# Two transformer blocks with expert layers: the gates' one-hots in token pairs, and every gate through DRAM

## The chip, the cores and the metric

One NeuronCore of one Trainium2 chip runs the whole program in one launch. Its engines work side by side, each through its own queue in order: TensorE (PE, with its weight loads PEld) multiplies matrices into PSUM, VectorE (DVE) and ScalarE (ACT) work elementwise on SBUF and PSUM, GpSimd (POOL) on SBUF, and SyncE (SP) and ScalarE issue DMAs. The metric is the device time of one execution in microseconds; before the change it is 2398.7 us, the median of 3 runs (2398.04 to 2399.11).

## What is computed

Two transformer blocks over 256 tokens of width 1024. The change lies in the expert layer of the second block, which runs twice (`li` = 0 and 1):

```python
def peer(h, wq, keys, u_tab, v_tab):           # for each block of 128 tokens
    q = (hblk @ wq).reshape(PEER_BLOCK, P_HEADS, 2, D_KEY_HALF)
    s = jnp.einsum('nhpd,hpkd->nhpk', q, keys)
    top_s, top_i = lax.top_k(s, P_TOPK)         # 16 of 128, for two halves of 8 heads
    cand_s = (top_s[:, :, 0, :, None] + top_s[:, :, 1, None, :]).reshape(...)
    cand_i = (top_i[:, :, 0, :, None] * N_KEYS + top_i[:, :, 1, None, :]).reshape(...)
    best_s, best_pos = lax.top_k(cand_s, P_TOPK)
    idx = jnp.take_along_axis(cand_i, best_pos, axis=-1)
    gate = jax.nn.softmax(best_s, axis=-1)
    act = jax.nn.gelu(jnp.einsum('nd,nhkd->nhk', hblk, u_tab[idx]))
    return jnp.einsum('nhk,nhkd->nd', gate * act, v_tab[idx])
```

Each token picks 16 experts of 128 x 128 = 16384 for each of 8 heads.

## The kernel before

Instead of gathering rows of U and V, the kernel multiplies the whole tables. The 16384 experts are 128 tiles of 128: tile `e` holds the experts of one first index, the second index lies on the partitions. For a **U tile** (`a_tile`, L1441) TensorE multiplies a 128 x 1024 tile of U with all 256 tokens, in 8 pieces of 128 rows; for a **V tile** (`v_tile`, L1468) it multiplies the gated activations of 128 experts with a 128 x 1024 tile of V into four PSUM banks `acc`. Between them lies `A[g]`, eight groups of 16 tiles: Gelu (L1453) writes it, the gates are multiplied into it, `w_pair` (L1459) splits two tiles of it for the V matmuls.

Everything is done in split precision: `hilo` (L200 to L202) makes a high half on ScalarE (L201) and a low half on VectorE or GpSimd (L202), and each product is three matmuls (L225 to L227 for U, with 256 columns; L242, L244, L246 for V, with 512). A weight tile is loaded on SP into one of 5 `raw` buffers (L197), split into one of 3 `hi` and `lo` buffers two tiles ahead, then used. `_plan` fixes the order of the tiles, U 0 to 111, V 0 to 15, U 112 to 127, V 16 to 127, and says which are split on GpSimd ("pool"): of U the five in `U_POOL0`.

**Gates** are dense: for each token a 128 x 128 matrix of gate values over first and second index, made of its 128 picks (they lie on the partitions) as a product of two one-hots. `g_hot` (L1379) takes four tokens: one VectorE instruction (L1382) compares the picks' two indices with `iota4`, a second (L1384) multiplies the first one-hot with the gate's high and low f16 part. Its tile has the order (kind, index, token), so that the columns of one token's one-hot lie four f16 apart. `g_mm` multiplies (L1392, L1393: for each of 4 tokens a high and a low product of 128 columns, both with the same weights). `g_out` evicts: first indices 0 to 63 stay in SBUF, 64 to 127 go to the DRAM tile `gspill` over ScalarE's DMA queue (L1406). `g_times` (L1408) multiplies gates into `A`.

**What sets the order** is a list by hand. Work for VectorE is put on `fill_q` with a cost in credits; after each tile `fill(budget)` adds a budget (at most 4.0 is kept) and runs entries while the credit is positive; `fill_all` runs what is left. In the Q stage (nine calls with 2.6) top-16 entries of 2.1 come in, 16 in all. Then `queue_topk` adds candidates (2.0 and 0.5), 8 times best of 1.4, 0.3, 18 pick steps of 1.8 (`pick_eq` on VectorE L1329 and GpSimd L1331, `pick_sum` L1334), decode 2.5 and transposes 0.5. U tiles 1 to 63 give 1.6 each and carry these; U tiles 64 to 111 give 2.75 and carry 67 gate steps of 1.9 (`queue_g0`: step i makes one-hots i, multiplies i - 1, evicts i - 2, and every second step multiplies 8 tokens of the first half into `A`); V tiles 16 to 63 carry 17 steps that read `gspill` back, 16 tokens each, and multiply the second half. In layer 0 `pump` also advances a generator that loads modulation rows (`ada`, L320 on VectorE, 512 KB each; its input row holds a `t4` buffer): after every second tile from U tile 36 to 63, of V 0 to 15, U 112 to 127 and V 64 to 111. `t4` has 4 buffers of 4 KB a partition; one-hots, rows read back and long-lived rows share them.

Of the kernel before, what the change touches and what calls it, by code (L numbers as in the profile page):

```python
# [19 lines left out]
P = 128  # L20
# [60 lines left out]
def _plan(t):  # L81
# [10 lines left out]
    for li in range(2):  # L92
# [7 lines left out]
        def u(a, b):  # L100
            return [(("u", li, e), t["u"][li, e], "pool" if e in U_POOL or e in U_POOL0 else None) for e in range(a, b)]

        def v(a, b, offload=()):
            return [(("v", li, e), t["v"][li, e], "pool" if e in offload else BIG[e % 2] if e >= P - TAIL else None) for e in range(a, b)]

        p += u(0, 112) + v(0, 16) + u(112, 128) + v(16, 64, V_POOL) + v(64, 128)
# [14 lines left out]
U_POOL0 = (2, 5, 8, 11, 14)  # L121
U_POOL = ()
V_POOL = ()
# [3 lines left out]
def tile_two_blocks(ctx: ExitStack, tc: tile.TileContext, t: dict, taps=None):  # L127
# [470 lines left out]
    gspill = p_dr.tile([P, NTOK, 64], F32, name="gspill")  # L598
# [422 lines left out]
    iota4 = const.tile([P, P, 4], F16, name="iota4")  # L1021
# [67 lines left out]
    vec.tensor_copy(out=iota4, in_=iota_f.rearrange("p (i n) -> p i n", n=4))  # L1089
# [143 lines left out]
    def peer(li, hT, zacc, mod, before_a, ada_next, after):  # L1233
# [13 lines left out]
        pk16 = p_pk.tile([P, 4, NTOK], F16, tag="pk16", name="pk16")  # L1247
# [107 lines left out]
        def picks_T():  # L1355
            for q, src in enumerate([i12[:, 0:256], i12[:, 256:512], gt.rearrange("p h k -> p (h k)")]):
# [3 lines left out]
                act.activation(out=pk16[:, q, :], in_=b, func=AF.Copy)  # L1360
                if q == 2:
                    vec.tensor_tensor(out=pk16[:, 3, :], in0=b, in1=pk16[:, 2, :], op=OP.subtract)
# [16 lines left out]
        def g_hot(i):  # L1379
            sl = slice(i * 4, i * 4 + 4)  # L1380
            o = t4(2048, F16).rearrange("p (q i n) -> p q i n", i=P, n=4)
            vec.tensor_tensor(out=o[:, 0:2], in0=pk16[:, 0:2, sl].unsqueeze(2).to_broadcast([P, 2, P, 4]),  # L1382
                              in1=iota4.unsqueeze(1).to_broadcast([P, 2, P, 4]), op=OP.is_equal)
            vec.tensor_tensor(out=o[:, 2:4], in0=o[:, 0].unsqueeze(1).to_broadcast([P, 2, P, 4]),  # L1384
                              in1=pk16[:, 2:4, sl].unsqueeze(2).to_broadcast([P, 2, P, 4]), op=OP.mult)
            held["hot", i] = o

        def g_mm(i):
            o = held.pop(("hot", i))
            b = mm([P, 4, P])  # L1390
            for n in range(4):
                pe.matmul(b[:, n, :], lhsT=o[:, 1, :, n], rhs=o[:, 2, :, n], start=True, stop=False)  # L1392
                pe.matmul(b[:, n, :], lhsT=o[:, 1, :, n], rhs=o[:, 3, :, n], start=False, stop=True)  # L1393
            held["g", i] = b

        def g_out(i):
            b = held.pop(("g", i))
            if i % 2 == 0:
                held["gs"] = [s1(512).rearrange("p (n i) -> p n i", i=64) for _ in range(2)]
            for c in range(2):  # L1400
                act.activation(out=held["gs"][c][:, i % 2 * 4:i % 2 * 4 + 4, :], in_=b[:, :, c * 64:c * 64 + 64],  # L1401
                               func=AF.Copy, scale=1.0 / GSC)
            if i % 2 == 1:
                gs = held.pop("gs")
                held["g0", i // 2] = gs[0]
                adma(out=gspill[:, i * 4 - 4:i * 4 + 4, :], in_=gs[1])  # L1406

        def g_times(g, c, n0, n):  # L1408
            for gg in range(4):
                ag = grp(c * 4 + gg)[:, :, n0:n0 + n]  # L1410
                vec.tensor_tensor(out=ag, in0=g[:, :, gg * 16:gg * 16 + 16].rearrange("p n i -> p i n"), in1=ag,
                                  op=OP.mult)

        def queue_g0():
            def step(i):
# [4 lines left out]
                if 2 <= i <= 65:  # L1420
                    g_out(i - 2)
                if i >= 4 and i % 2 == 0:
                    g_times(held.pop(("g0", i // 2 - 2)), 0, i * 4 - 16, 8)
# [339 lines left out]
```

## Time and profile before

| | |
|---|---|
| median of 3 runs | 2398.7 us |
| the profiled execution, its own time | 2398.1 us |
| its span, first to last instruction | 2396.2 us |
| PE, PEld busy | 2284.1, 2029.0 us |
| DVE, ACT, POOL busy | 1838.3, 1170.7, 315.5 us |
| mean granted TensorE clock | 0.992 |
| HBM | 475.67 MB read, 19.97 MB written |

The profile counts an engine busy while an instruction of it runs. Matmuls overlap in their pipeline, so a TensorE that is busy throughout can still be slow: how fast it goes is read from the number of matmuls in a stretch and from the distance of their starts. A bracket behind an instruction gives the idle time of its engine before it and what ended it.

### The profile page before, as it was taken

The numbers are of one execution on the slowest core, as the hardware profiler recorded it, in microseconds if no ns is written. First come the engines' busy times: TensorE is split into PE (matmuls) and PEld (weight loads), VectorE is DVE, ScalarE is ACT, GpSimd is POOL, SyncE is SP. The second block draws the span as 40 slices with busy tenths as digits, with TensorE's granted clock in tenths as the row PEclk, the third lists the DMA queues.
The fourth block names the chain that finished last, engine by engine and source line by source line (L and its number), as shares of the span: only waits on it lengthen the run. The fifth ranks groups of instructions, "written<-read, shape, count | busy, mean of one in ns | idle before, by whom it ended". The sixth has DMA issues, their size and how long they took to land. (4 is left out here: it accounts for less than half of the span.)

```text
span 2396.2 us, 37336 instructions
## 1 busy us (share of the span) xinstructions
PE 2284.1 (95%) x14334; PEld 2029.0 (85%) x14334; DVE 1838.3 (77%) x3188; ACT 1170.7 (49%) x1821; POOL 315.5 (13%) x202
## 2 busy tenths in 40 slices
PE   6988899989999999999999999999999999999998
PEld 4668888866798999998888887899899998988886
DVE  5989877646699779987786777789849995587556
ACT  4663444357454545544444445554444554444443
POOL 2234401120333000000000003144200000000001
PEclk8989999999999999999999999999999999999999
DMA  8556776621564765457886886545555555686664
GB/s 325 202 205 232 248 274 234 224 82 61 175 192 154 260 227 174 161 174 284 285 275 227 291 305 212 198 165 166 169 183 168 168 168 184 210 276 224 193 211 150
DMA packets 143074, 498.08 MB, mean 208 GB/s; under 512 B 15824, under 2 KB 18416, under 8 KB 142768
## 3 DMA queue, kind: packets, MB, share of 16 engines
q1 hardware_dynamic: 133648, 478.89, 59.7%
q10 hardware_dynamic: 9248, 16.81, 1.9%
q8 instruction: 112, 1.84, 0.3%
q14 instruction: 66, 0.54, 0.1%
HBM read 475.67 MB, written 19.97 MB: 207 GB/s over the span
## 5 line engine op out<-in xcount | busy, mean ns | idle before, releaser
L202 DVE TENSOR_TENSOR lo<-raw,hi 128x1024 fp32r<-128x1024 f32 x611 | 784.5, 1287 | 402.4 <-ACT hi L201 400.6
L201 ACT ACTIVATE hi<-raw 128x1024 fp32r<-128x1024 f32 x668 | 705.6, 1059 | 788.5 <-PE mm L246 383.4
L227 PE MATMUL mm<-hTh,lo 128*128 128x256 f32 x2592 | 739.3, 285 | 31.1 <-DVE lo L202 16.4
L225 PE MATMUL mm<-hTh,hi 128*128 128x256 f32 x2592 | 745.3, 288 | 0.7 <-ACT hTh L419 0.7
L226 PE MATMUL mm<-hTl,hi 128*128 128x256 f32 x2592 | 735.1, 284 | 0.2 <-DVE hTl L421 0.2
L227 PEld LDWEIGHTS mm<-hTh,lo 128*128 128x128 f32 x2592 | 497.8, 192 | 39.8 <-DVE lo L202 21.3
L225 PEld LDWEIGHTS mm<-hTh,hi 128*128 128x128 f32 x2592 | 499.6, 193 | 4.0 <-issue 2.6
L226 PEld LDWEIGHTS mm<-hTl,hi 128*128 128x128 f32 x2592 | 498.6, 192 | 0.7 <-POOL hTl L421 0.5
L242 PE MATMUL mm<-hi,s 128*128 128x512 f32 x992 | 306.1, 390 | 4.8 <-ACT s L201 4.8
L244 PE MATMUL mm<-lo,s 128*128 128x512 f32 x992 | 305.6, 389 | 0.9 <-DVE lo L202 0.9
L246 PE MATMUL mm<-hi,s 128*128 128x512 f32 x992 | 305.4, 389 | 0.0
L202 POOL TENSOR_TENSOR lo<-raw,hi 128x1024 fp32r<-128x1024 f32 x57 | 151.1, 2653 | 1008.5 <-ACT hi L201 979.3
L242 PEld LDWEIGHTS mm<-hi,s 128*128 128x128 f32 x992 | 185.8, 188 | 44.1 <-ACT s L201 5.6
L244 PEld LDWEIGHTS mm<-lo,s 128*128 128x128 f32 x992 | 186.1, 188 | 40.1 <-DVE lo L202 1.4
L246 PEld LDWEIGHTS mm<-hi,s 128*128 128x128 f32 x992 | 186.1, 188 | 38.9 <-DVE s L202 0.3
L1401 ACT ACTIVATE s<-mm 128x256 f32<-128x256 f32 x256 | 84.1, 384 | 120.6 <-PE mm L1393 120.4
L1392 PE MATMUL mm<-t 128*128 128x128 f16 x512 | 126.0, 295 | 1.5 <-DVE t L1384 1.5
L1393 PE MATMUL mm<-t 128*128 128x128 f16 x512 | 126.9, 297 | 0.0
L429 POOL TENSOR_TENSOR sm<-sm,mhalf 128x1 f32<-128x1 f32 (+1 forms) x18 | 11.5, 640 | 780.0 <-DVE sm L428 779.9
L320 DVE SCALAR_TENSOR_TENSOR raw<-raw,t 128x1024 f32<-128x1024 f32 x84 | 104.6, 1247 | 4.8 <-DMA raw<-in_ada_dram 4.8
L1384 DVE TENSOR_TENSOR t<-t,pk 128x1024 f16<-128x1024 f16 x128 | 88.6, 692 | 4.4
L202 DVE TENSOR_TENSOR s<-big,s 128x512 fp32r<-128x512 f32 x126 | 86.3, 685 | 6.2 <-ACT s L201 6.2
(283 smaller groups left out, 2818.7 us busy)
## 6 DMA issues: line engine op xcount, KB each, us to landing
raw<-in_u_dram SPq DMA_DIRECT2D x256, 512.0 KB, 3.6
raw<-in_v_dram SPq DMA_DIRECT2D x256, 512.0 KB, 4.2
raw<-in_ada_dram SPq DMA_DIRECT2D x124, 512.0 KB, 4.5
raw<-in_ffn_in_dram SPq DMA_DIRECT2D x44, 512.0 KB, 4.5
raw<-in_ab_in_dram SPq DMA_DIRECT2D x32, 512.0 KB, 5.2
gspill<-s ACTq DMA_DIRECT2D x64, 256.0 KB, 2.0
t<-gspill SPq DMA_DIRECT2D x32, 512.0 KB, 5.4
raw<-in_ffn_out_dram SPq DMA_DIRECT2D x22, 512.0 KB, 4.9
```

The source lines that it names most:

```text
L201: act.activation(out=hi, in_=src, func=AF.Copy)
L202: (eng or vec).tensor_tensor(out=lo, in0=src, in1=hi.bitcast(F32), op=OP.subtract)
L225: pe.matmul(out, lhsT=sh, rhs=mh, start=(i == 0), stop=False)
L226: pe.matmul(out, lhsT=sh, rhs=ml, start=False, stop=False)
L227: pe.matmul(out, lhsT=sl, rhs=mh, start=False, stop=(i == n - 1))
L242: pe.matmul(o[c], lhsT=sh[:, tk], rhs=wh[:, cs[c]], start=first, stop=False)
L244: pe.matmul(o[c], lhsT=sh[:, tk], rhs=wl[:, cs[c]], start=False, stop=False)
L246: pe.matmul(o[c], lhsT=sl[:, tk], rhs=wh[:, cs[c]], start=False, stop=last)
L320: vec.scalar_tensor_tensor(out=o, in0=r, scalar=1.0, in1=c, op0=OP.mult, op1=OP.mult, accum_out=m[:, j:j + 1])
L1384: vec.tensor_tensor(out=o[:, 2:4], in0=o[:, 0].unsqueeze(1).to_broadcast([P, 2, P, 4]), in1=pk16[:, 2:4, sl].unsqueeze(2).to_broadcast([P, ...
L1392: pe.matmul(b[:, n, :], lhsT=o[:, 1, :, n], rhs=o[:, 2, :, n], start=True, stop=False)
L1393: pe.matmul(b[:, n, :], lhsT=o[:, 1, :, n], rhs=o[:, 3, :, n], start=False, stop=True)
```

## The change

All 128 first indices of the gates now go to DRAM, in blocks of 8 tokens, and come back in 32 reads a layer, each 16 first indices of 64 tokens; a read's runs in DRAM are 16 x 8 values, 512 bytes. `g_hot` still takes four tokens, as two pairs, so that the columns of one token's one-hot lie two f16 apart. `g_out` is one eviction of 512 values with the token innermost, in place of two of 256. Gate steps (66 of 1.5) follow the picks at once on `fill_q`, and all U tiles 1 to 111 give 1.45. Behind them, still on `fill_q`, stand four reads and four products of group 0 (8 entries of 0.7); at U tile 110 `fill_all` and the split of V tiles 0 and 1 follow. The other 28 products stand beside V (`g_next`), one every fourth tile, each read one step ahead; `w_pair(8)` is moved to U tile 126. No U tile is split on GpSimd. `pump` runs after every fourth U tile from 36 on, not beside V 0 to 15, and after every third V tile from 16 to 111.

```diff
         def u(a, b):
-            return [(("u", li, e), t["u"][li, e], "pool" if e in U_POOL or e in U_POOL0 else None) for e in range(a, b)]
...
-        def v(a, b, offload=()):
-            return [(("v", li, e), t["v"][li, e], "pool" if e in offload else BIG[e % 2] if e >= P - TAIL else None) for e in range(a, b)]
...
-        p += u(0, 112) + v(0, 16) + u(112, 128) + v(16, 64, V_POOL) + v(64, 128)
+            return [(("u", li, e), t["u"][li, e], None) for e in range(a, b)]
...
+        def v(a, b):
+            return [(("v", li, e), t["v"][li, e], BIG[e % 2] if e >= P - TAIL else None) for e in range(a, b)]
...
+        p += u(0, 112) + v(0, 16) + u(112, 128) + v(16, 128)
...
-U_POOL0 = (2, 5, 8, 11, 14)
-U_POOL = ()
-V_POOL = ()
+G_STEP = 1.5
...
-    gspill = p_dr.tile([P, NTOK, 64], F32, name="gspill")
+    gspill = p_dr.tile([P, NTOK // 8, P, 8], F32, name="gspill")
...
-    iota4 = const.tile([P, P, 4], F16, name="iota4")
+    iota2 = const.tile([P, P, 2], F16, name="iota2")
...
-    vec.tensor_copy(out=iota4, in_=iota_f.rearrange("p (i n) -> p i n", n=4))
+    vec.tensor_copy(out=iota2, in_=iota_f.rearrange("p (i n) -> p i n", n=4)[:, :, 0:2])
...
-        pk16 = p_pk.tile([P, 4, NTOK], F16, tag="pk16", name="pk16")
...
+        pk16 = p_pk.tile([P, 2, NTOK // 2, 2, 2], F16, tag="pk16", name="pk16")
...
                     pe.transpose(b[:, hf * P:hf * P + P], src[:, hf * P:hf * P + P], ident)
-                act.activation(out=pk16[:, q, :], in_=b, func=AF.Copy)
+                b = b.rearrange("p (a n) -> p a n", n=2)
+                act.activation(out=pk16[:, q // 2, :, q % 2, :], in_=b, func=AF.Copy)
                 if q == 2:
-                    vec.tensor_tensor(out=pk16[:, 3, :], in0=b, in1=pk16[:, 2, :], op=OP.subtract)
+                    vec.tensor_tensor(out=pk16[:, 1, :, 1, :], in0=b, in1=pk16[:, 1, :, 0, :], op=OP.subtract)
...
         def g_hot(i):
-            sl = slice(i * 4, i * 4 + 4)
-            o = t4(2048, F16).rearrange("p (q i n) -> p q i n", i=P, n=4)
-            vec.tensor_tensor(out=o[:, 0:2], in0=pk16[:, 0:2, sl].unsqueeze(2).to_broadcast([P, 2, P, 4]),
-                              in1=iota4.unsqueeze(1).to_broadcast([P, 2, P, 4]), op=OP.is_equal)
-            vec.tensor_tensor(out=o[:, 2:4], in0=o[:, 0].unsqueeze(1).to_broadcast([P, 2, P, 4]),
-                              in1=pk16[:, 2:4, sl].unsqueeze(2).to_broadcast([P, 2, P, 4]), op=OP.mult)
-            held["hot", i] = o
+            o = t4(2048, F16)
+            pk = pk16[:, :, i * 2:i * 2 + 2]
+            o12 = o[:, 0:1024].rearrange("p (a i n) -> p a i n", i=P, n=2)
+            vec.tensor_tensor(out=o12, in0=pk[:, 0].rearrange("p a q n -> p (a q) n").unsqueeze(2).to_broadcast([P, 4, P, 2]),
+                              in1=iota2.unsqueeze(1).to_broadcast([P, 4, P, 2]), op=OP.is_equal)
+            o1 = o12.rearrange("p (a q) i n -> p a q i n", q=2)[:, :, 0:1]
+            vec.tensor_tensor(out=o[:, 1024:2048].rearrange("p (a q i n) -> p a q i n", q=2, i=P, n=2),
+                              in0=o1.to_broadcast([P, 2, 2, P, 2]), in1=pk[:, 1].unsqueeze(3).to_broadcast([P, 2, 2, P, 2]),
+                              op=OP.mult)
+            held["hot", i] = o.rearrange("p (s a q i n) -> p s a q i n", s=2, a=2, q=2, n=2)
...
         def g_mm(i):
             o = held.pop(("hot", i))
             b = mm([P, 4, P])
             for n in range(4):
-                pe.matmul(b[:, n, :], lhsT=o[:, 1, :, n], rhs=o[:, 2, :, n], start=True, stop=False)
-                pe.matmul(b[:, n, :], lhsT=o[:, 1, :, n], rhs=o[:, 3, :, n], start=False, stop=True)
+                a, m = divmod(n, 2)
+                for q in range(2):
+                    pe.matmul(b[:, n, :], lhsT=o[:, 0, a, 1, :, m], rhs=o[:, 1, a, q, :, m], start=q == 0, stop=q == 1)
             held["g", i] = b
...
         def g_out(i):
             b = held.pop(("g", i))
             if i % 2 == 0:
-                held["gs"] = [s1(512).rearrange("p (n i) -> p n i", i=64) for _ in range(2)]
-            for c in range(2):
-                act.activation(out=held["gs"][c][:, i % 2 * 4:i % 2 * 4 + 4, :], in_=b[:, :, c * 64:c * 64 + 64],
-                               func=AF.Copy, scale=1.0 / GSC)
+                held["gs"] = t4().rearrange("p (i n) -> p i n", n=8)
+            act.activation(out=held["gs"][:, :, i % 2 * 4:i % 2 * 4 + 4], in_=b.rearrange("p n i -> p i n"), func=AF.Copy,
+                           scale=1.0 / GSC)
             if i % 2 == 1:
-                gs = held.pop("gs")
-                held["g0", i // 2] = gs[0]
-                adma(out=gspill[:, i * 4 - 4:i * 4 + 4, :], in_=gs[1])
...
-        def g_times(g, c, n0, n):
-            for gg in range(4):
-                ag = grp(c * 4 + gg)[:, :, n0:n0 + n]
-                vec.tensor_tensor(out=ag, in0=g[:, :, gg * 16:gg * 16 + 16].rearrange("p n i -> p i n"), in1=ag,
-                                  op=OP.mult)
...
-        def queue_g0():
+                adma(out=gspill[:, i // 2], in_=held.pop("gs"))
...
+        def queue_g():
             def step(i):
                 if i < 64:
                     g_hot(i)
                 if 1 <= i <= 64:
                     g_mm(i - 1)
-                if 2 <= i <= 65:
+                if 2 <= i:
                     g_out(i - 2)
-                if i >= 4 and i % 2 == 0:
-                    g_times(held.pop(("g0", i // 2 - 2)), 0, i * 4 - 16, 8)
...
-            for i in range(67):
-                fill_q.append((1.9, lambda i=i: step(i)))
...
-        def queue_g1():
-            def step(i):
-                if i < 16:
-                    held["g1", i] = t4().rearrange("p (n i) -> p n i", i=64)
-                    dma(out=held["g1", i], in_=gspill[:, i * 16:i * 16 + 16, :])
-                if i >= 1:
-                    g_times(held.pop(("g1", i - 1)), 1, i * 16 - 16, 16)
...
-            for i in range(17):
-                fill_q.append((1.5, lambda i=i: step(i)))
...
+            for i in range(66):
+                fill_q.append((G_STEP, lambda i=i: step(i)))
...
+        def g_read(k):
+            g, h = divmod(k, 4)
+            held["gr", k] = t4().rearrange("p (b i n) -> p b i n", b=8, n=8)
+            dma(out=held["gr", k], in_=gspill[:, h * 8:h * 8 + 8, g * 16:g * 16 + 16, :])
...
+        def g_times(k):
+            g, h = divmod(k, 4)
+            ag = grp(g)[:, :, h * 64:h * 64 + 64].rearrange("p i (b n) -> p b i n", n=8)
+            vec.tensor_tensor(out=ag, in0=held.pop(("gr", k)), in1=ag, op=OP.mult)
...
+        def queue_g0():
+            for i in range(8):
+                fill_q.append((0.7, lambda i=i: [1 < i < 6 and g_read(i - 2), i > 3 and g_times(i - 4)]))
...
+        def g_next(e):
...
+            if e == 0:
+                g_read(4)
+            if e % 4 == 1 and e < 112:
+                if e < 109:
+                    g_read(e // 4 + 5)
+                g_times(e // 4 + 4)
...
         queue_topk()
-        for e in range(1, 64):
+        queue_g()
+        queue_g0()
+        for e in range(1, 112):
             a_tile(e)
-            fill(1.6)
+            fill(1.45)
+            if e == 110:
+                fill_all()
+                w_pair(0)
...
-                pump(e % 2)
-        fill_all()
-        queue_g0()
-        for e in range(64, 112):
-            a_tile(e)
-            fill(2.75)
+                pump(e % 4 == 1)
         a_flush()
-        fill_all()
         acc = [mm([P, 512]) for _ in range(4)]
         for e in range(16):
+            g_next(e)
...
-            pump(e % 2)
         for e in range(112, 128):
             a_tile(e)
             pump(e % 2)
+            if e == 126:
+                w_pair(8)
         a_flush()
-        queue_g1()
         for e in range(16, 64):
-            v_tile(e, e < 62)
-            fill(0.65)
-        fill_all()
+            g_next(e)
+            v_tile(e)
+            pump(e % 3 == 0)
         for e in range(64, 128):
...
+            g_next(e)
             v_tile(e)
...
-                pump(e % 2)
+                pump(e % 3 == 0)
```

## Rows read from the trace of the kernel before

**Rows 1.** Busy time on the page: engine, us, share of the span, instructions.

```profile
PE 2284.1 (95%) x14334; PEld 2029.0 (85%) x14334; DVE 1838.3 (77%) x3188; ACT 1170.7 (49%) x1821; POOL 315.5 (13%) x202
```

**Rows 2.** Stretches: us, busy per engine (instructions), granted clock, DMA share, GB/s.

```profile
680.00:700.00 20.00, 20.00 (x169) 20.00 (x168) 19.98 (x102) 10.09 (x12) 6.08 (x3) 1.00 0.60 185
...
740.00:760.00 20.00, 17.93 (x144) 17.22 (x144) 20.00 (x17) 7.81 (x9) 9.45 (x6) 1.00 0.48 156
...
800.00:820.00 20.00, 20.00 (x169) 20.00 (x168) 13.49 (x16) 9.71 (x12) 0.00 (x0) 1.00 0.86 316
900.00:920.00 20.00, 20.00 (x170) 19.69 (x170) 18.52 (x33) 9.19 (x20) 0.00 (x0) 1.00 0.53 172
...
1180.00:1200.00 20.00, 20.00 (x90) 16.57 (x89) 18.04 (x26) 9.63 (x11) 0.00 (x0) 1.00 0.84 282
1260.00:1280.00 20.00, 20.00 (x90) 16.57 (x89) 13.67 (x16) 9.78 (x12) 0.00 (x0) 1.00 0.63 195
```

**Rows 3.** Waits, 720 to 800 us: waiting line, waited for: us, times, longest.

```profile
PEld mm L227 <- DVE lo L202: 10.1, 11, 1.6
```

**Rows 4.** Order of time at the first gate matmuls: start, duration (us), instruction, count.

```profile
872.19 0.11 PEld L1392 LDWEIGHTS <-t 128*128 128x128 f16 x1 [0.95 <-DVE t L1384]
872.21 0.13 PEld L1393 LDWEIGHTS <-t 128*128 128x128 f16 x1
...
872.20 0.28 PE L1392 MATMUL mm<-t 128*128 128x128 f16 x1 [0.74 <-DVE t L1384]
872.30 0.30 PE L1393 MATMUL mm<-t 128*128 128x128 f16 x1
872.42 0.30 PE L1392 MATMUL mm<-t 128*128 128x128 f16 x1
```

**Rows 5.** Groups by line: count, then us busy in all, mean ns.

```profile
L202 DVE TENSOR_TENSOR lo<-raw,hi 128x1024 fp32r<-128x1024 f32 x611 | 784.5, 1287 | 402.4 <-ACT hi L201 400.6
...
L1384 DVE TENSOR_TENSOR t<-t,pk 128x1024 f16<-128x1024 f16 x128 | 88.6, 692 | 4.4
...
L1453 ACT ACTIVATE big<-mm 128x512 f32<-128x512 f32 x128 | 74.7, 584 | 7.8 <-PE mm L227 7.8
```

**Rows 6.** Order of time in the pick steps, VectorE and GpSimd (columns as in 4).

```profile
750.66 0.98 DVE L1329 TENSOR_TENSOR big<-big,kst 128x800 f32<-128x800 f32 x1
751.56 0.97 DVE L1334 TENSOR_REDUCE big<-big 128x16 f32<-128x800 f32 x1
751.72 1.76 POOL L1331 TENSOR_TENSOR big<-big 128x800 f32<-128x800 f32 x1 [2.06 <-DVE big L1329]
752.46 2.10 DVE L202 TENSOR_TENSOR lo<-raw,hi 128x1024 fp32r<-128x1024 f32 x1
...
767.75 3.23 DVE L202 TENSOR_TENSOR lo<-raw,hi 128x1024 fp32r<-128x1024 f32 x2
```

**Rows 7.** DMA issues: count, KB each, median us from issue to landing.

```profile
raw<-in_u_dram SPq DMA_DIRECT2D x256, 512.0 KB, 3.6
...
gspill<-s ACTq DMA_DIRECT2D x64, 256.0 KB, 2.0
t<-gspill SPq DMA_DIRECT2D x32, 512.0 KB, 5.4
```

**Rows 8.** Order of time at the turn from U to V (columns as in 4).

```profile
1069.20 0.62 ACT L201 ACTIVATE s<-big 128x512 fp32r<-128x512 f32 x1
...
1069.88 0.73 PE L242 MATMUL mm<-hi,s 128*128 128x512 f32 x2 [1.21 <-ACT s L201]
```

**Rows 9.** Stretches around a pause of TensorE early on (columns as in 2).

```profile
153.00:159.00 6.00, 0.32 (x2) 0.00 (x0) 5.97 (x16) 2.39 (x7) 2.10 (x3) 0.95 0.01 2
160.00:166.00 6.00, 4.29 (x16) 2.79 (x15) 3.28 (x10) 5.91 (x18) 3.54 (x5) 0.50 0.35 99
```

**Rows 10.** DMA queues on the page: packets, MB, share of 16 engines' span.

```profile
q1 hardware_dynamic: 133648, 478.89, 59.7%
q10 hardware_dynamic: 9248, 16.81, 1.9%
```

## The prediction

> **What bounds the kernel now.** First the busy totals on the page, then the table of 20 us stretches through the first expert layer (U tiles from 676 us, V tiles from 1069 us; the second layer repeats it some 918 us later), then the waits, and last the order of time at three places. TensorE is busy 95% of the span [rows 1]. In the stretches of U and V tiles it is at 20.00 of 20 [rows 2], with one exception in the U tiles: between 720 and 800 us it falls to 17.93, while VectorE is at 20.00. The waits there say why: the weight loads of L227 waited 11 times, 10.1 us in all, for the low half that VectorE makes [rows 3]. So the expert layers are TensorE's, and only in the pick steps VectorE's.
>
> A U tile is 24 matmuls, one every 0.12 us: 2.88 us. In the gate stretch the table counts 170 matmuls in 20 us, in the pure U stretch 169 [rows 2]: a gate matmul of 128 columns takes TensorE as long (0.118 us) as a U matmul of 256. There are 64 steps of 8 of them in a layer, 1024 in all: 1024 x 0.119 = 122 us, 5% of the time.
>
> **Part 1: pairs instead of fours.** Both one-hots of a gate matmul are read every fourth f16 (8 bytes apart); with pairs every second one (4 bytes apart, as dense f32r columns lie). What spaces the matmuls? Not the weight load alone: after the pause of 0.95 us at 871 us the first load starts at 872.19 and the second 0.02 later, yet the second matmul follows the first by 0.10 and the rest by 0.12 [rows 4]. So the moving stream looks like the slow part, at twice the time for a column of a 256-column f32r matmul. From 512 columns at 20/90 = 0.222 us and 256 at 20/169 = 0.118 [rows 2], 0.104 is 256 columns and 0.014 is fixed: 128 columns at full rate would be 0.066; with the 0.02 of a weight load that doesn't overlap, 0.086. Bounds therefore 0.066 and 0.119 (no row has the pair form; a narrower step can't read more, so a loss is excluded). I take 0.075, near the first, since dense f32r is the nearest form in bytes: 1024 x (0.119 - 0.075) = 45 us saved, on TensorE itself and so on the path. By bounds, 0 to 54.
>
> One page speaks for less, one against. The Trainium skill, TensorE: Matmul & The Clock Gate, section Back-to-back issue gap, gives a stream of weight loads and 128-column matmuls about 81 ns each; by that, as an estimate, the saving is 1024 x 38 ns = 39 us and the time some 6 us later; no run here shows it yet. The Trainium skill, SBUF - State Buffer, section Door 1: The DMA port swizzle, says that SBUF has lines of 16 bytes, that two hits in a line suffice, and that a step of up to 8 two-byte elements is free. By that rule fours are free already and pairs buy nothing; the 0.118 us of [rows 4] don't show what slows them, so this is a rival below.
>
> VectorE's two instructions keep 1024 elements each (692 ns now [rows 5]), with rows of 2 in place of 4. Bound: no change to the 1287 ns of a 1024-element f32 instruction [rows 5]; I take no change. ScalarE evicts once with 512 elements in place of two times 256; nearest is the Gelu eviction of 512, 584 ns [rows 5], and at worst, reading tokens 2 KB bank columns apart, twice that. ScalarE is at 9 of 20 [rows 2], so either is hidden; cover gone, it would cost 64 x 0.4 = 26 us in a layer.
>
> **Part 2: GpSimd splits no U tile.** Five splits a layer come to VectorE: 5 x 1.14 us (a second one in a row adds 3.23 - 2.10 [rows 6]). There VectorE is at 19.98 of 20 (680 to 700 us [rows 2]), but each tile gets 1.45 of fill in place of 1.6: over the 18 tiles before the picks 2.7 us less. Net some 3 us more work, which eats the cushion of two tiles that are split ahead; nothing of it need reach TensorE.
>
> **Part 3: picks over more tiles.** A pick step is 0.90 + 0.90 us on VectorE, and the next split takes 2.10 beside GpSimd's product of 1.76 [rows 6]: 3.83 a round, against 2.88 of TensorE. 18 steps at 1.8 took 20 tiles, 2 of them without one: 18 x 3.83 + 2 x 1.14 = 71.2 against 57.6, 13.6 short; 10.1 was waited, so the cushion is 3.5. At 1.45 they take 22 tiles, 4 without: 73.5 against 63.4, 10.1 short, 6.6 waited. I take 3 us gained in a layer (bounds -2, if part 2 uses the cushion up, to 7).
>
> **Part 4: gates over tiles 43 to 110.** 66 steps of 1.5 at 1.45: one a tile. VectorE then has 1.14 + 0.97 x 1.35, with the ada row of every fourth tile 0.29: 2.7 us against TensorE's 2.88 + 0.97 x 0.6 = 3.4. No wait; the 0.95 us before the first gate matmul [rows 4] goes, since its one-hot is a tile old. The products move from 192 pieces of 128 and 256 elements to 32 of 1024: less VectorE time, where it wasn't the bound.
>
> **Part 5: the turn to V.** This is the new wait. The credits before it are 6 x 2.1 (the top-16 entries that the Q stage leaves over), 49.4 (candidates, best, picks, decode) and 99 (gates), 161 in all, and 110 tiles give 159.5: the last gate step runs in the flush at tile 110, and all reads and products of group 0 with it. V tile 0 needs group 0 multiplied for all 256 tokens, so the last tokens' gates go TensorE, ScalarE, DRAM, SP, VectorE, ScalarE, while TensorE has only tile 111. From the end of tile 110: gate matmuls 0.85, eviction 0.8 (between 0.58 and 1.1), issue 0.35; landing 3.0 (256 KB takes 2.0; now 512 KB, whose loads take 3.6 [rows 7]); SP 0.4; read back 4.5 (between 3.6 and 5.4 [rows 7]); product 1.2; high half of the weights 0.62 [rows 8]. Together 11.7. TensorE is free at 0.6 + 2.88 = 3.5, so it stands 8.2 us; now the same turn costs 1.2 [rows 8]: 7 more. In layer 0 the modulation row holds one of the four t4 buffers, so read 2 waits on SP for the last write too and shares the DMA engines with read 3: 2 more, 9. Behind SP's wait are V loads, but three V tiles are loaded by then; behind ScalarE's wait for the product are the next splits, needed a V tile later. Bounds: 4 (quick landings) to 14 (all four reads wait for the last write).
>
> The stop may cost clock: after a stretch in which TensorE was busy 0.32 of 6.00 us the granted clock was 0.50 from 160 to 166 us [rows 9], 1.2 GHz, with a full stream at half speed. I take 2.5 us a turn (0 to 6). The second turn, today like the first, vanishes, since its weights are split at tile 126: 1.2 gained.
>
> **Part 6: gates beside V.** 28 reads of 512 KB a layer, one every four V tiles, in 512-byte pieces, on SP ahead of V loads; their buffers are free a round before. V alone is 195 GB/s; with a read every third tile 282, still 20.00 of TensorE; 316 GB/s were held at 800 us [rows 2]. Layer 0 also loads modulation rows every third tile: 195 x (1 + 1/3 + 1/4) = 309. Halving the pieces cost nothing (2 KB on q10, 16.81 MB at 1.9%, is 1.13% for 10 MB; q1, 478.89 MB at 59.7%, 1.25% [rows 10]). If 512 bytes cost double, 357 against 316: 96 tiles x 2.7 x 0.13 = 34 us. I take 2.
>
> **The sum** against the profiled execution's own 2398.1 us (span 2396.2 and 1.9 around it; 0.6 below the median of 2398.7, which I leave): gates -45; picks -3 and first gate -0.9, twice: -7.8; turns +9 +7, clock +5, second turns -2.4, V stage +2: +20.6. Together -32.2: 2366 us.
>
> **Rivals.** *A: the step of a gate matmul isn't set by the byte distance* (a floor of the f16 form, say). Then -45 is 0 and the turn decides: 2398.1 + 12.8 = 2411, slower. It decides as soon as a gate matmul saves under 12.8/1024 = 12.5 ns, a step over 0.106 us. For it: loads and matmuls are paired one by one at 0.12 [rows 4], and a floor would look alike. Against: the early second load. (The SBUF page of the Trainium skill gives a rule of this kind, above.) *B: VectorE or the DMA engines become the bound*: rows of 2 at 1.29 us make VectorE 1.14 + 0.97 x 2.4 + 0.29 = 3.8 a tile against 3.4 in layer 0, 68 x 0.4 = 25 us; or the 34 us above: about 2390. Against: 16-bit rows of 4 run at 692 ns, half the f32 time, so runs this short don't hurt. *C: the turn is cheaper*, quick landings and no clock loss: 2366 - 12 - 9 (at 0.066) = 2345.
>
> **Chances.** Forecast 0.68, own range 2345 to 2387; A 0.22; B 0.06; C 0.04. The range, 2340 to 2412, goes to A's value and leaves out A's upper half and little else. A measurement of this kernel tells 0.2% (4.8 us) from no change. Faster 0.77 (forecast, B, C); same 0.06 (A with a cheap turn); slower 0.17 (the rest of A).
>
> **What would show it.** Starts of gate matmuls 0.066 to 0.086 apart (right) or 0.118 (A). One TensorE gap of 6 to 11 us before V tile 0 in each layer, ended by ScalarE's high half, with the clock at 0.50 behind it. Waits of L227 for VectorE near 7 us in a layer. V tiles at 90 matmuls in 20 us. Wrong would be: no gap (the reads don't wait), or V tiles spread out in layer 0.

## The result, and the profile after

The changed kernel takes **2357.6 us** (median of 4 runs, 2355.4 to 2360.0) beside 2398.9 us of the kernel before (the median of four runs; the 2398.7 ahead of the prediction is that of three of them): a ratio of 0.983, interval 0.981 to 0.985, 41 us faster. The forecast was 2366 us in a range of 2340 to 2412. The profiled execution took 2355.4 us with a span of 2353.7, 42.5 us under the span before.

The page of the changed kernel: the busy totals, and four groups of instructions by line (count, then us busy in all, mean ns of one, idle time of the engine before them and what ended it), and two groups of DMA issues (count, KB each, median us to landing). They answer to [rows 1], [rows 5] and [rows 7].

```profile
PE 2232.6 (95%) x14334; PEld 1979.1 (84%) x14334; DVE 1773.6 (75%) x2878; ACT 1158.7 (49%) x1693; POOL 290.8 (12%) x192
...
L240 PE MATMUL mm<-hi,s 128*128 128x512 f32 x992 | 307.7, 391 | 19.7 <-ACT s L199 19.7
...
L1404 ACT ACTIVATE t<-mm 128x512 f32<-128x512 f32 x128 | 75.5, 590 | 61.4 <-DMA gspill<-t 51.8
...
L1386 DVE TENSOR_TENSOR t<-t,pk 128x1024 f16<-128x1024 f16 x128 | 88.6, 692 | 4.4
L1429 DVE TENSOR_TENSOR big<-t,big 128x1024 f32<-128x1024 f32 x64 | 78.1, 1220 | 14.7 <-DMA t<-gspill 14.7
...
gspill<-t ACTq DMA_DIRECT2D x64, 512.0 KB, 3.3
t<-gspill SPq DMA_DIRECT2D x64, 512.0 KB, 5.3
```

TensorE has the same 14334 matmuls in 51.5 us less. The one-hots kept their 692 ns with rows of two, and the eviction, which reads its bank with the tokens 512 bytes apart, takes 590 ns, where the Gelu eviction of [rows 5] takes 584. New are 19.7 us in which V's first matmuls waited for ScalarE's high half, and 51.8 us in which the eviction waited for earlier gates to land in DRAM, all of them in layer 0.

The stretches of the changed kernel (columns as in [rows 2]): start of the U tiles, picks, gates, the turn to V in layer 0, and V.

```profile
680.00:700.00 20.00, 19.43 (x160) 19.03 (x159) 20.00 (x88) 9.45 (x12) 0.00 (x0) 1.00 0.51 163
740.00:760.00 20.00, 18.58 (x150) 17.86 (x148) 20.00 (x17) 8.79 (x10) 8.83 (x5) 1.00 0.46 152
900.00:920.00 20.00, 20.00 (x187) 19.79 (x186) 14.69 (x18) 9.84 (x15) 0.00 (x0) 1.00 0.77 257
...
1046.00:1052.00 6.00, 0.07 (x1) 0.07 (x1) 3.04 (x4) 0.75 (x2) 0.00 (x0) 0.50 1.08 316
1052.00:1056.00 4.00, 4.00 (x10) 3.13 (x11) 3.54 (x4) 2.77 (x4) 0.00 (x0) 0.50 1.07 317
...
1180.00:1200.00 20.00, 20.00 (x90) 16.57 (x89) 14.91 (x18) 9.75 (x12) 0.00 (x0) 1.00 0.91 313
1260.00:1280.00 20.00, 20.00 (x90) 16.57 (x89) 15.75 (x18) 9.18 (x11) 0.00 (x0) 1.00 0.93 306
```

Of the four things to see: the gate stretch now holds 187 matmuls in 20 us in place of 170, with VectorE at 14.7 in place of 18.5; the picks still wait; at the turn TensorE stands and then runs 10 matmuls in 4 us at a granted clock of 0.50; V keeps its 90 matmuls with the DMA engines at 0.91 to 0.93.

The order of time at one gate step of layer 1 (start, duration, instruction, count; eight matmuls of one line are one row):

```profile
1901.59 0.28 PE L225 MATMUL mm<-hTh,lo 128*128 128x256 f32 x1
1901.70 0.46 PEld L1397 LDWEIGHTS <-t 128*128 128x128 f16 x8
1901.71 0.63 PE L1397 MATMUL mm<-t 128*128 128x128 f16 x8
...
1902.15 0.36 PE L223 MATMUL mm<-hTh,hi 128*128 128x256 f32 x1
...
1902.35 0.28 PE L224 MATMUL mm<-hTl,hi 128*128 128x256 f32 x1
```

One takes 0.22 (the mean of its line), so their starts lie (0.63 - 0.22)/7 = 0.059 us apart; the median over all is 0.057, where [rows 4] has 0.12. The U matmul behind them is 0.08 late (0.20 to the next start in place of 0.12), so this step costs 1902.35 - 1901.59 - 0.24 = 0.52 us. Over the 64 steps of layer 1 it is (229.7 - 68 x 2.88)/64 = 0.53 (the 229.7 from the table below), 0.066 a matmul.

The order of time at the turn, layer 1 without its matmuls of U (the bracket: idle time of the engine before, and what ended it), ahead of it the four reads and the first V matmul of layer 0. It answers to [rows 8].

```profile
1037.36 8.15 SPq L1424 DMA_DIRECT2D t<-gspill  x4
...
1051.93 1.22 PE L240 MATMUL mm<-hi,s 128*128 128x512 f32 x2 [11.60 <-ACT s L199]
...
1935.19 0.63 PE L1397 MATMUL mm<-t 128*128 128x128 f16 x8
1935.85 6.01 SPq L1424 DMA_DIRECT2D t<-gspill  x2
1935.86 0.60 ACT L1404 ACTIVATE t<-mm 128x512 f32<-128x512 f32 x1 [1.96 <-PE mm L1397]
...
1936.49 0.33 ACTq L1407 DMA_DIRECT2D gspill<-t  x1
...
1944.95 1.22 DVE L1429 TENSOR_TENSOR big<-t,big 128x1024 f32<-128x1024 f32 x1 [1.99 <-DMA t<-gspill]
1946.21 0.63 ACT L199 ACTIVATE s<-big 128x512 fp32r<-128x512 f32 x1 [9.75 <-DVE big L1429]
...
1946.89 1.22 PE L240 MATMUL mm<-hi,s 128*128 128x512 f32 x2 [8.15 <-ACT s L199]
```

The chain of layer 1 can be read down the start times: last gate matmuls at 1935.19, eviction, write, the last read leaving SP at 1941.86, product, high half, V.

The starts of the first matmul of a tile, taken from both traces, say where the 42 us went (us; "before to after"):

| stretch | layer 0 | layer 1 | both | predicted |
|---|---|---|---|---|
| U 0 to U 43: picks | 136.9 to 133.8 | 136.9 to 133.7 | -6.3 | -6 |
| U 43 to U 111: gates | 257.7 to 232.6 | 257.6 to 229.7 | -53.0 | -46.8 |
| U 111 to V 0: the turn | 4.2 to 14.7 | 4.2 to 11.3 | +17.5 | +16 |
| V 0 to U 112: clock | 43.7 to 45.6 | 43.7 to 45.3 | +3.6 | +5 |
| U 112 to V 16: second turn | 47.4 to 46.1 | 47.4 to 46.1 | -2.7 | -2.4 |
| the rest, V 16 to 127 among it | | | -1.6 | +2 |

Together -42.5, the difference of the two spans; -32.2 was predicted.

### The profile page after: what moved, and what is told of

It reads as the page before. It is cut to its first block, busy times and chain, and to the rows that moved or that the text cites. A ratio compares the mean times of both kernels' runs of the same rounds, so it can differ in the third digit from the quotient of the medians.

```text
span 2353.7 us, 36890 instructions
## 1 busy us (share of the span) xinstructions
PE 2232.6 (95%) x14334; PEld 1979.1 (84%) x14334; DVE 1773.6 (75%) x2878; ACT 1158.7 (49%) x1693; POOL 290.8 (12%) x192
## 5 line engine op out<-in xcount | busy, mean ns | idle before, releaser
L200 DVE TENSOR_TENSOR lo<-raw,hi 128x1024 fp32r<-128x1024 f32 x621 | 795.4, 1284 | 417.2 <-ACT hi L199 416.2
L240 PE MATMUL mm<-hi,s 128*128 128x512 f32 x992 | 307.7, 391 | 19.7 <-ACT s L199 19.7
L200 POOL TENSOR_TENSOR lo<-raw,hi 128x1024 fp32r<-128x1024 f32 x47 | 122.1, 2600 | 922.0 <-ACT hi L199 884.4
L1404 ACT ACTIVATE t<-mm 128x512 f32<-128x512 f32 x128 | 75.5, 590 | 61.4 <-DMA gspill<-t 51.8
L1429 DVE TENSOR_TENSOR big<-t,big 128x1024 f32<-128x1024 f32 x64 | 78.1, 1220 | 14.7 <-DMA t<-gspill 14.7
L199 ACT ACTIVATE s<-big 128x512 fp32r<-128x512 f32 x126 | 77.3, 614 | 22.9 <-DVE big L1429 22.9
L318 DVE SCALAR_TENSOR_TENSOR raw<-raw,big 128x1024 f32<-128x1024 f32 x40 | 81.1, 2028 | 8.7 <-DMA raw<-in_ada_dram 8.1
```

Source lines behind the costliest of these rows:

```text
L199: act.activation(out=hi, in_=src, func=AF.Copy)
L200: (eng or vec).tensor_tensor(out=lo, in0=src, in1=hi.bitcast(F32), op=OP.subtract)
L240: pe.matmul(o[c], lhsT=sh[:, tk], rhs=wh[:, cs[c]], start=first, stop=False)
L318: vec.scalar_tensor_tensor(out=o, in0=r, scalar=1.0, in1=c, op0=OP.mult, op1=OP.mult, accum_out=m[:, j:j + 1])
L1404: act.activation(out=held["gs"][:, :, i % 2 * 4:i % 2 * 4 + 4], in_=b.rearrange("p n i -> p i n"), func=AF.Copy, scale=1.0 / GSC)
L1429: vec.tensor_tensor(out=ag, in0=held.pop(("gr", k)), in1=ag, op=OP.mult)
```

## The experiments

The theory: the byte distance of the moving columns sets the step of a gate matmul; the pairs earn all of the gain; the turn gives part of it back, by the chain through DRAM. Against it stand rival A (the step has another cause), and for each loss a second cause.

### Fours put back

```diff
-            for n in range(4):
-                a, m = divmod(n, 2)
-                for q in range(2):
-                    pe.matmul(b[:, n, :], lhsT=o[:, 0, a, 1, :, m], rhs=o[:, 1, a, q, :, m], start=q == 0, stop=q == 1)
+                pe.matmul(b[:, n, :], lhsT=o[:, 1, :, n], rhs=o[:, 2, :, n], start=True, stop=False)
+                pe.matmul(b[:, n, :], lhsT=o[:, 1, :, n], rhs=o[:, 3, :, n], start=False, stop=True)
```

(and `g_hot`, `iota4` and `pk16` as before)

> The changed kernel with the layout of fours put back (one-hot columns 8 bytes apart); placement, DRAM round and turn stay as changed. Theory, the byte distance sets the step: gate matmuls start 0.118 us apart again; a gate step of 8 cost 0.967 us of TensorE before and 0.531 after (from the time between U tiles 43 and 111 less 68 tiles of 2.88), so 64 x 0.436 = 27.9 us in each layer come back, less some 3 us of eviction waits in layer 0 that the slower steps would hide: 2357.6 + 53 = 2411 us, slower than the kernel before. Rival, the placement of the steps made them quicker: the step stays near 0.057 and the time near 2358.

Measured: 2406.9 us (2403.0 to 2409.3), ratio to before 1.0033, interval 1.0021 to 1.0044; the gate matmuls lie 0.12 apart again (rows of that trace):

```profile
1902.80 0.28 PE L1391 MATMUL mm<-t 128*128 128x128 f16 x1
...
1902.90 0.30 PE L1392 MATMUL mm<-t 128*128 128x128 f16 x1
...
1903.02 0.30 PE L1391 MATMUL mm<-t 128*128 128x128 f16 x1
...
1903.14 0.30 PE L1392 MATMUL mm<-t 128*128 128x128 f16 x1
```

All of the change but the pairs costs 8 us; the pairs are worth 2406.9 - 2357.6 = 49 us in it. The time is near that of rival A (2411), as it must be: the same sum with 0 for the step.

### The pairs alone

The kernel before, with `iota2`, `pk16`, `g_hot` and `g_mm` of the change.

> The kernel before with the pair layout alone. Theory: the step falls to 0.057 us, but in the 48 U tiles that carry the gates VectorE was busy 18.1 of 20 us, 3.87 us of the 4.28 of a tile with its 1.45 steps; TensorE would now need 2.88 + 1.45 x 0.531 = 3.65, so VectorE becomes the bound: some 47 x 0.41 = 19 us gained in a layer, 2398.9 - 38 = 2361 us, with waits of the U weight loads for VectorE's low half in the gate stretch. Rival, TensorE stays the bound: 2 x 27.9 = 56 us gained, 2343 us, no such waits.

Measured: 2365.1 us (2364.0 to 2365.8), ratio 0.986, interval 0.984 to 0.988. Two stretches of the gates (columns as in [rows 2]):

```profile
900.00:920.00 20.00, 19.76 (x190) 19.20 (x190) 19.76 (x36) 11.45 (x25) 0.00 (x0) 1.00 0.57 186
920.00:940.00 20.00, 17.67 (x176) 16.93 (x175) 19.72 (x35) 11.09 (x24) 0.00 (x0) 1.00 0.57 193
```

TensorE's wait there, from 880 to 1060 us (line, waited for: us, times, longest):

```profile
PE mm L1398 <- DVE t L1387: 9.1, 11, 1.2
```

VectorE is at 19.7 and TensorE waits for it, as the theory said, though for the one-hots and not for the low half of U. So the pairs earn 33 us in the kernel before, with the gates in 48 tiles and VectorE as the bound, and 49 us in the changed one, with the gates in 68. How much of the 16 us between them is the spreading alone, no run singles out.

### Which operand, and which distance

Three kernels keep everything and only let the gate matmuls read with other distances.

```diff
-                    pe.matmul(b[:, n, :], lhsT=o[:, 0, a, 1, :, m], rhs=o[:, 1, a, q, :, m], start=q == 0, stop=q == 1)
+                    pe.matmul(b[:, n, :], lhsT=col(0, sw, n * 2), rhs=col(1, sm_, n * 2 + q), start=q == 0, stop=q == 1)
```

with `col(z, s, j)` 128 columns, s elements apart.

> The changed kernel whose gate matmuls read the same one-hot buffers with other distances: step i takes its weights' columns 1, 2, 4 or 8 f16 apart (by i // 4 % 4) and the moving columns 1, 2, 4 or 8 apart (by i % 4), so the gates are not the reference's. Theory, the moving operand's byte distance sets the step up to a floor: moving 1 and 2 give 0.057 us whatever the weights, moving 4 gives 0.118, moving 8 twice that (0.236) if the cost goes on with the distance or 0.118 if it is a threshold. Rival 1, the weight load's distance sets it: the rows by weights differ and those by moving don't. Rival 2, both: 4 in either gives 0.118. One look at the trace; the total is of no use.

Measured, median ns from one start to the next (56 steps in each field):

| weights apart | moving 1 | 2 | 4 | 8 |
|---|---|---|---|---|
| 1 | 56 | 59 | 115 | 227 |
| 2 | 56 | 57 | 115 | 230 |
| 4 | 56 | 60 | 118 | 230 |
| 8 | 62 | 64 | 123 | 235 |

Four steps of that trace, weights dense, moving 1, 2, 4 and 8 apart; eight matmuls in a row:

```profile
878.57 0.62 PE L1402 MATMUL mm<-t 128*128 128x128 f16 x8
...
881.95 0.64 PE L1402 MATMUL mm<-t 128*128 128x128 f16 x8
...
885.35 1.08 PE L1402 MATMUL mm<-t 128*128 128x128 f16 x8
...
889.15 1.98 PE L1402 MATMUL mm<-t 128*128 128x128 f16 x8
```

The moving operand alone sets the step, and it goes on growing: pairs are at the floor, fours at twice it. The weights' distance costs some 6 ns at 8 and at most 3 below. Both rivals fall. A second table asks for the shape of the curve and for f32r, the type of the U and V matmuls (the profile prints it as f32):

> As the first table of steps, with ten forms in turn (by i % 10; the gates are not the reference's): f16 with moving columns 2, 3, 5, 6 and 16 apart (4, 6, 10, 12 and 32 bytes), weights 16 apart (32 bytes), and in place of the one-hots f32r columns of the U stage's own input, dense (4 bytes), moving 2 and 4 apart (8 and 16 bytes), weights 2 apart. Theory, the moving operand is read at 4 bytes a column and its step grows with the byte distance above that, whatever the type: from 57 ns at 4 bytes and 115 at 8, 14.4 ns a byte, so 6 bytes 86, 10 bytes 144, 12 bytes 172, 32 bytes 460; f32r 8 bytes 115 and 16 bytes 230. Rival, distances count in elements: f32r 2 apart is as quick as f16 2 apart, equal to f32r dense. Weights 32 bytes apart: 62 at 16 bytes; between 62 (hidden) and 124.

Measured for f16: 57 at 2 apart, 84 at 3, 143 at 5, 171 at 6, as the theory has it; but 232 at 16, no more than at 8. Weights 16 apart: 63. For f32r: 111 dense, 116 at 2, 118 at 4, where the theory wanted 230. One step each of f16 6 and 16 apart and f32r 4 apart:

```profile
1790.76 1.53 PE L1406 MATMUL mm<-t 128*128 128x128 f16 x8
...
1798.50 2.01 PE L1406 MATMUL mm<-t 128*128 128x128 f16 x8
...
1814.62 1.11 PE L1406 MATMUL mm<-hTh 128*128 128x128 f32 x8
```

So "bytes, whatever the type" falls, and both types got a third table with 256 columns:

> Again the changed kernel with other operands for the gate matmuls (ten forms in turn, the gates are not the reference's): f32r columns of the U stage's input, 256 of them 1, 2, 4 and 8 apart, 128 of them 8 and 16 apart; f16 columns, 256 of them 1, 2, 4 and 8 apart; weights dense. The second table had f32r at 118 ns with columns 16 bytes apart, where f16 took 228, so bytes alone don't set it. Theory now, elements: 0.224 ns a column for each element of distance, from 2 (f16) on, at most 8; then 256 f32r columns 2 apart take 118, 4 apart 230, 8 apart 457, and 128 of them 8 apart 228. Rival, f32r is read in another way and its distance costs nothing up to here: 118 in all forms of 256, 111 to 118 in those of 128. f16, 256 columns: 111 to 118 at 1 and 2 apart, 230 at 4, 457 at 8.

Measured: f32r 120, 227, 233, 218 at 1, 2, 4 and 8 apart (128 columns 8 and 16 apart: 110 and 113); f16 109, 114, 227, 451. Steps of f32r dense, 2 and 4 apart, and f16 4 apart:

```profile
1822.89 1.12 PE L1402 MATMUL mm<-hTh 128*128 128x256 f32 x8
...
1826.73 1.98 PE L1402 MATMUL mm<-hTh 128*128 128x256 f32 x8
...
1831.42 2.03 PE L1402 MATMUL mm<-hTh 128*128 128x256 f32 x8
...
1855.86 1.98 PE L1402 MATMUL mm<-t 128*128 128x256 f16 x8
```

Neither elements (f32r 2 apart would be 118) nor "costs nothing" holds. What the tables do say, with 256 columns: both types run at full pace up to 4 bytes and at half of it at 8 bytes; f16 goes on to a quarter at 16 bytes (and, with 128 columns, stays there at 32), f32r stays at half. Why f32r stops at half is open. The forms of 128 f32r columns show little of the distance: dense they take 111 ns already, nearly the 120 of 256 columns, so something other than the columns holds them. No run shows what; a weight load takes 0.19 us there, in f16 0.10.

### The turn, by a smaller price for gate steps

```diff
-G_STEP = 1.5
+G_STEP = 1.3
```

> The changed kernel with gate steps priced 1.3 credits in place of 1.5: the last step then falls at U tile 102 and the products of group 0 at tiles 105 and 106, no longer into the flush at tile 110. Theory, the stall before V tile 0 is the chain from the last gates through DRAM: it goes (10.4 us in layer 0, 7.0 in layer 1), and with it the slow V matmuls behind it (1.9 and 1.7): 2357.6 - 21 = 2337 us. Rival, the reads land late because the DMA engines are busy there, or VectorE waits for them ahead of the U splits: at least half of it stays, 2347 us or more, as a gap of TensorE in U tiles 104 to 111 that ends on VectorE's low half.

Measured: 2337.9 us (2334.2 to 2341.8), ratio 0.974, interval 0.972 to 0.976. U 111 to V 0 takes 2.9 us in both layers and V 0 to U 112 43.5: stall and slow clock are gone together. Layer 1 does what was expected; in the trace, which is of the longest of the four runs (2341.8 us), the gate stretch of layer 0 takes 10 us more than in the changed kernel (U 43 to U 110 239 in place of 229), with these waits between 805 and 1051 us:

```profile
ACT t L1404 <- DMA gspill<-t: 68.5, 25, 5.8
...
PE mm L1397 <- DVE t L1386: 7.0, 7, 1.5
PE mm L225 <- DVE lo L200: 2.7, 1, 2.7
```

A smaller dose, 1.45:

> The changed kernel with gate steps priced 1.45: the last step falls at U tile 108, read 0 at tile 110, and reads 1 to 3 and all products of group 0 stay in the flush. Theory, the stall is a chain of two halves (last gates written, then read back, multiplied and split): the first half now lies two tiles earlier and is covered, the second is not. From the end of tile 110: some 0.4 until the last read is issued, 5.4 to land, 1.2 product, 0.6 high half, 7.6 us, less 3.5 of tile 111 and the rest of tile 110: a stall of about 4 us in both layers in place of 10.4 and 7.0, 2357.6 - 6.5 - 3 - 2 of clock = 2346 us. Rival 1, only the writes matter: the stall is gone, 2337 us as with 1.3. Rival 2, only the reads matter: nothing changes, 2357.

Measured: 2342.7 us (2342.0 to 2343.7), ratio 0.977, interval 0.975 to 0.978. The first V matmul of layers 0 and 1:

```profile
1046.05 0.79 PE L240 MATMUL mm<-hi,s 128*128 128x512 f32 x1 [7.60 <-ACT s L199]
...
1935.12 0.73 PE L240 MATMUL mm<-hi,s 128*128 128x512 f32 x2 [2.35 <-ACT s L199]
```

Part of the stall stays, as a chain of two halves predicts, and neither rival's time is met. The 4 us were 7.6 and 2.4, unequal between the layers; that layer 0 has three `t4` buffers for four reads would explain it, but no run singles it out. Nearly 3 us of the gain over the changed kernel are of another kind: in this trace the gate stretch of layer 0 loses nothing (U 43 to U 111 229.8 in both layers, where the changed kernel had 232.6 and 229.7). Behind the stop of 7.6 us V 0 to U 112 took 45.7, behind that of 2.4 us 43.7, as without a stop.

### Buffers of their own for the evicted gates

```diff
-                held["gs"] = t4().rearrange("p (i n) -> p i n", n=8)
+                held["gs"] = [s1(512).rearrange("p (i n) -> p i n", n=8) for _ in range(2)]
```

(with `G_STEP` 1.3; two evictions and two writes, each half of the first indices)

> The kernel with gate steps of 1.3, whose evicted gates lie in two tiles of the s1 pool (two evictions of 256 and two writes of 256 KB in 2 KB runs a step pair), no longer in a t4 buffer. Theory, the 7.9 us that TensorE waits before gate matmuls in layer 0 (none in layer 1) come from t4: the modulation row holds one of four, so one-hots and evictions wait until a written buffer is free. With buffers of their own these waits go and layer 0 takes the time of layer 1 in its gate stretch: 2337.9 - 8 = 2330 us. Rival, the modulation loads fill the DMA engines and the writes land late whatever holds them: the eviction still waits for the write, time 2336 to 2340.

Measured: 2331.4 us (2330.6 to 2332.4), ratio 0.972, interval 0.970 to 0.974; 6.5 us under the kernel with `G_STEP` 1.3 alone, whose own runs lie 7.6 us apart. TensorE waits for nothing in the gate stretch of layer 0; this row is of the kernel with `G_STEP` 1.3 alone (columns as in [rows 2]):

```profile
900.00:920.00 20.00, 18.46 (x178) 18.03 (x177) 17.61 (x24) 10.48 (x16) 0.00 (x0) 1.00 0.89 285
```

The same stretch with buffers of their own:

```profile
900.00:920.00 20.00, 20.00 (x193) 19.79 (x191) 17.70 (x23) 11.64 (x23) 0.00 (x0) 1.00 0.89 293
```

The DMA engines are as busy as without (0.89) and the writes land no sooner, though they are half as large (median 3.6 us, 3.5 without), so the wait was for the buffer, not for the engines.

### The GpSimd splits put back

```diff
-            return [(("u", li, e), t["u"][li, e], None) for e in range(a, b)]
+            return [(("u", li, e), t["u"][li, e], "pool" if e in U_POOL0 else None) for e in range(a, b)]
```

> The changed kernel with the five U tiles of U_POOL0 split on GpSimd again. In the changed kernel U tiles 0 to 19 took 1.7 us (layer 0) and 2.2 us (layer 1) more than before. Theory, that is VectorE's five splits: those waits go, and with a full cushion the picks lose no more than now: U tiles 0 to 42 in all 1.5 to 2 us quicker in each layer, 2357.6 - 3.5 = 2354 us. Rival, the cushion of split tiles is used up by the picks in either case and the waits only move: U tile 43 starts where it does now, 2357.

Measured: 2354.0 us (2352.1 to 2354.7), 3.5 under the changed kernel; U 0 to U 43 takes 131.6 and 131.3 us in place of 133.8 and 133.7. The waits didn't only move. (The runs of the changed kernel lie 4.6 us apart, so these starts show it better than the time.)

### All four

> Gate steps of 1.3, evicted gates in buffers of their own, the five GpSimd splits back, and fill 1.35 up to U tile 46 and 1.6 behind it (picks over 24 tiles, gates from tile 47 to 99, products of group 0 by tile 103). Theory: 2330 as with the gates' own buffers, 3.5 for the splits, and picks with 18 x 3.83 + 6 x 1.14 = 75.8 against 69.1 of TensorE, 6.7 short less the cushion of 3.5, 3.2 waited in place of 6.6: 7 in both layers. 2330 - 3.5 - 7 = 2320 us. Rival, VectorE has too much in the gate stretch at 1.23 steps a tile (1.22 + 1.23 x 1.38 + 0.31 = 3.2 of 3.53 us) to refill the cushion, and what is won in the picks is waited there: 2327 to 2330.

Measured: **2324.2 us** (2323.5 to 2325.3), ratio 0.969, interval 0.967 to 0.971: faster than both kernels. From the 2331.4 us of the gates' own buffers 7 of the expected 10.5 us came; U 0 to U 43 takes 129.3 and 128.2. TensorE's waits between 670 and 825 us:

```profile
PE mm L226 <- DVE lo L201: 3.0, 5, 0.7
PE mm L1398 <- DVE t L1387: 1.2, 1, 1.2
```

In the picks the matmuls waited 3.0 us and the weight loads, in which the expectation is counted, 4.4 where it had 3.2; and a first gate step waits for its one-hot: the pause of [rows 4] is back. U 0 to U 43 won 10 us on the kernel with the gates' own buffers (133.8 and 133.7 there), and U 43 to U 111 gave 4.3 of it back (231.8 and 231.4 in place of 229.5 and 229.4): the last of the picks, now behind tile 43, and this pause. The rest of the gate stretch holds (VectorE 18.3 of 20 at 900 us), so the rival, a cushion that isn't refilled, is not seen.

## Why the prediction was right, and where it wasn't

- **Part 1, the pairs: the mechanism was right, the size too small.** The starts lie 0.059 us apart, below the lower bound of 0.066; that a gate matmul costs 0.066 after all comes of its share of the late U matmul, which the prediction didn't have, so the bound was met by luck. 0.075 was taken: 1024 x 0.009 = 9 us more than the sum had, of which layer 0 lost 2.9 again (part 4); that is 6 of the 10 us by which the sum fell short. The term that was off is the choice inside the bounds: the 0.02 us for a weight load that doesn't overlap was half counted, and no weight load showed. That dense f32r is the nearest form in bytes was borne out for 256 columns up to 8 bytes. It wasn't for 128, the form at hand: the bound was carried down from f32r matmuls of 512 and 256 columns, and 128 dense f32r columns take 0.111 us in the second table, so the same reasoning would have failed for one-hots in f32r. Of the pages: the Trainium skill, TensorE: Matmul & The Clock Gate, section Back-to-back issue gap, gives about 81 ns for a load and a matmul of 128 columns; the trace has 59 in runs of eight, and 66 with the U matmul behind. The Trainium skill, SBUF - State Buffer, section Door 1: The DMA port swizzle, lets a step of 8 two-byte elements go free; for the moving operand the tables show twice the time at 4 and four times at 8, so the measurement decides against it here, and with it against rival A.
- **VectorE and ScalarE in part 1:** no change, as taken (692 and 590 ns; the tokens lie 512 bytes apart in their bank, not 2 KB).
- **Parts 2 and 3: the sum right by two errors that cancel.** -6 was predicted, -6.3 measured; but the five splits, costed at nothing, took 2.2 and 2.4 us on TensorE, and the picks over more tiles alone gained 5.3 and 5.6 a layer (U 0 to U 43 with the splits back, against before), not 3. The cover that was named, the cushion of two tiles, was gone at once: TensorE's first wait came at 684 us, in the stretch where [rows 2] had VectorE at 19.98 of 20. The weight loads waited 7.5 and 7.4 us a layer, near the 7 that were named, but in layer 0 1.6 of it came before the picks. A stretch without slack doesn't hide what is added to it.
- **Part 4: "no wait" was wrong in layer 0.** The evictions had been moved into `t4`, where the modulation row holds one of four buffers. The prediction saw that for the reads of the turn and not for the 32 writes of a layer: 2.9 us of TensorE there, and 12.8 in the trace with `G_STEP` 1.3 (242.1 against 229.4 us from U 43 to U 111), but nothing in that with 1.45; why the size differs so is open. The first gate's 0.95 us went, as said.
- **Part 5, the turn: the wait was right, its size by errors that cancel.** It stood 8.15 us in layer 1, 8.2 predicted, and 11.6 in layer 0, 10.2 predicted. The terms were less good than their sum: in layer 1 the write took 4.6 where 3.0 was taken (1936.82 to 1941.86 less the read's issue of 0.4), the read 3.1 where 4.5 was (to 1944.95). In layer 0 the last write took 6.7 us from issue to landing (1038.08 to 1044.74), and the last read, which needs it, left SP at 1045.51; the read ahead of it was sent only when the first product had given its buffer back (1044.52), a wait for `t4` as the prediction had named one, but the write is the longer term. The clock cost 1.9 and 1.6 for 2.5: it stood at 0.50 for some 9 us of the stop in layer 0 and 3.3 in layer 1, and in each for only some 4 us of V matmuls. The second turn went as said.
- **Part 6: nothing, where 2 was taken.** V holds 90 matmuls in 20 us at 313 GB/s in 512-byte pieces. Rival B is not seen in the changed kernel; it is what bounds the pairs alone. Of rival C the 0.066 came, the cheaper turn did not.

## What to carry to other kernels

Lay the moving operand of a matmul so that its columns lie at most 4 bytes apart; a one-hot interleaved by four cost twice the time of one interleaved by two, and the weights' layout next to nothing. When a faster step makes another engine the bound, spread the work over a longer stretch, then count the chain of waits at the end of that stretch: letting the gates end eight tiles earlier was worth 20 us here, by one constant. A buffer pool that one long-lived tile shares is a pool of one less, for every user that a change adds.

## What the runs showed of the hardware beside that

- A moving f16 operand of 256 columns runs at 0.43 to 0.45 ns a column up to 4 bytes apart, 0.89 at 8 and 1.76 at 16; 128 columns 32 bytes apart take 1.81; 256 f32r columns at 0.47 dense and 0.85 to 0.91 at 8 to 32 bytes.
- TensorE lost the clock without a pause, too. In the third table it was busy throughout, and yet behind eight matmuls 0.45 us apart the granted clock was 0.50 (1.2 GHz) for some 2.8 us, with the U matmuls 0.213 us apart, in 4 of 12 such places (the eight matmuls, then the stretch behind them, columns as in [rows 2]):

```profile
897.25:900.44 3.19, 3.19 (x10) 0.86 (x9) 1.99 (x3) 1.06 (x1) 0.00 (x0) 0.94 0.22 91
900.50:903.30 2.80, 2.80 (x14) 2.66 (x13) 1.78 (x4) 0.60 (x1) 0.00 (x0) 0.50 0.85 275
```

- ScalarE reads a PSUM bank with 512 bytes between neighbours nearly as fast as in a row (590 ns for the eviction, 584 for Gelu).
